# Encoder block in fp32 halves: output projection by token halves, FFN weight operands of four blocks kept in DRAM, a lead of six blocks

## The chip, the cores and the metric

The kernel runs on one core of one Trainium2 chip. The metric is the device time of one execution in microseconds, the median of several runs. PE is TensorE, DVE VectorE, ACT ScalarE, POOL GpSimd, and SP the engine that issues every DMA of this kernel, in order.

## The reference

One encoder layer on 1024 tokens of 1024 features, then a final norm. What the change touches is the middle of it:

```python
merged = gates[:, :, 0] * br_att + gates[:, :, 1] * br_sgu
h = h + merged @ w_out[l]
hn = rmsnorm(h, norm_ffn[l])
g, up = jnp.split(hn @ w_ffn_in[l], 2, axis=-1)
h = h + (jax.nn.silu(g) * up) @ w_ffn_out[l]
return rmsnorm(h, norm_final)
```

`w_out` is 1024 x 1024, `w_ffn_in` 1024 x 5632 (gate and up, 2816 columns each), `w_ffn_out` 2816 x 1024.

## The kernel before

Features lie on the 128 partitions, tokens along a row. A tile of 1024 features is 8 tiles of 128 (`KB`), a token half is 512 columns (`HALF`), and the FFN's 2816 columns are 22 blocks of 128 (`FB`).

**Products.** Every float32 operand is split into a high part (a cast by ACT into fp32r) and a low part (the difference, a subtraction by DVE or POOL). A product then is three matmuls of 128 x 128 by 128 x 512: high by high, high by low, low by high. `passes` (L158) and `multiply` (L175) issue them.

**The output projection** (L1193 to L1252) makes eight row blocks `j` of 128 features by two token halves: 16 products of 24 matmuls, in the hand-written order `order_w` (L1221), where halves alternate at first. `load_w` and `split_w` (L1034, L1039) fetch `w_out` and split it, half of the low parts on POOL and half on DVE. `collect_w` (L1202) adds the product to the residual row `h[j]` on DVE; `finish_row` (L1172) squares it on ACT and adds the square into `acc[half]`, mostly on POOL, and stores the row into `h_dram` once both halves are there. Once the eight rows of half 0 are collected, PE sums the squares (`sum_features`, L266), `inverse_rms` (L250) makes the reciprocal root with a power on POOL and three DVE instructions, and PE spreads it over the partitions (`spread`, L273) into `bc`. `first_operands` (L1214) then norms half 0 into `exact` and splits it into the right-hand operands `b11` and `b21`.

**The FFN's input product** uses seven products per block instead of eight (a Strassen-Winograd scheme over 2 x 2 halves: features by tokens on the right, features by gate and up on the left). `order` (L1109) lists them: products "1" and "2" use `b11` and `b21`, which come of token half 0 alone; "5", "6", "3", "7", "4" use `t1`, `t2`, `b22`, `t3`, `t4`, which need half 1 too. Products 1 and 2 of the first four blocks (`AHEAD`) lead, eight products; then the rest follows block by block, 154 products of 12 matmuls in all. `prepare_to(n)` (L1137) makes the weight operands up to product `n`: a combination on DVE for 5, 6, 3 and 7 (`combine`, L1132), a cast on ACT (L1156), and the low part on POOL (L1162) or, from block 4 on, for the products in `VECTOR_LO` on DVE (L173). They lie in four pairs of buffers of two products each, turn by turn in `fpool` and `wpool`. `load_raw` (L1119) fetches the raw rows.

The loop at L1400 goes through the products: it prepares four ahead, issues the product, and `collect` (L1272) takes it out of PSUM. Behind product 0 stand the sums of half 1, behind product 1 the spread; from then on `TAKE_F[i]` (L32) tells how many items of `other_operands` (L1314) follow product `i`. There are 20 items: four each for t1, t2, b22, t3 and t4, with a norm or difference on DVE, a cast on ACT and a low part, alternately on POOL and DVE (`put_later`, L1318).

**The FFN's output product** needs weight operands too, made early: `weights_g` (L1357) makes 84 of them during the input product, one item per product from `MAKE_FROM` (18) on, and keeps them in `g_dram`; they are loaded back later.

**Space.** `slots` (L58) has 36 buffers of 4 KB a partition for nearly everything. Tiles are allotted in program order, and an instruction that writes a reused buffer waits for its last user. PSUM has eight banks of 512 columns for products (`dense_ps`, L79). The order of each engine's work is the order of the program.

Of the kernel before, what the change touches and what calls it, by code (L numbers as in the profile page):

```python
# [16 lines left out]
P = 128  # L17
# [14 lines left out]
TAKE_F = (0, 2, 1, 2, 0, 2, 3, 2, 2, 4, 2, 1)  # L32
TAKE_G = (0, 2, 1, 1, 1, 3, 2, 2, 2, 2, 2, 1, 1, 1, 1, 1, 1, 2, 1, 1, 2, 0, 3)
POOL_LO = (0, 2, 6)
VECTOR_LO = "1247"
MAKE_FROM = 18
# [12 lines left out]
def encoder_block(ctx: ExitStack, tc: tile.TileContext, xT, w_in, w_v, w_vs, w_att, w_sgu, w_out,  # L49
# [984 lines left out]
    def load_w(j):  # L1034
        pool = wpool if j in (0, 2) else fpool if j in (4, 6) else None
        raws_w[j] = slot(f"wo{j}") if pool is None else pool.tile([P, D], F32, name=f"wo{j}", tag="raw")
# [71 lines left out]
    AHEAD = 4  # L1108
# [11 lines left out]
    def load_raw(f, i):  # L1120
        name = f"f{'gu'[i]}{f}"
        pool = (fpool, wpool)[i if f < 2 else 1 - f % 2]
        t = slot(name) if 2 <= f < AHEAD else pool.tile([P, D], F32, name=name, tag="raw")
        nc.sync.dma_start(t, w_ffn_in[i * FB + f])
        raws.setdefault(f, []).append(t)
# [11 lines left out]
    def prepare_to(n):  # L1137
        while state_f["next"] < min(n, len(order)):
            i = state_f["next"]
            p, f = order[i]  # L1140
            if i % 2 == 0:
                parts[i // 2] = weight_parts(f"w{i}", (fpool, fpool, wpool, wpool)[i // 2 % 4])
            (g0, g1), (u0, u1) = ((x[:, :HALF], x[:, HALF:]) for x in (raws[f][0], raws[f][-1]))
# [10 lines left out]
            c = slice(i % 2 * HALF, (i % 2 + 1) * HALF)  # L1154
            hi, lo = (x[:, c] for x in parts[i // 2])
# [7 lines left out]
            if (p, f) == ("7", 1):  # L1163
                load_pair(5)
            if p == "4" and (f == 1 or f > 3):
                load_pair(4 if f == 1 else f + 2)
            state_f["next"] += 1

    acc = [ftmp("acc0"), ftmp("acc1")]
    lazy = []  # L1170

    def finish_row(j, half, first=False, last=False):  # L1172
        x = h[j][:, halves[half]]
        if first:
            nc.scalar.activation(acc[half], x, AF.Square)
        else:
            q = tmp("sq")
            nc.scalar.activation(q, x, AF.Square)
            if last:
                do_lazy(99)  # L1180
            lazy.append(lambda: (nc.vector if last else nc.gpsimd).tensor_tensor(out=acc[half], in0=acc[half], in1=q, op=OP.add))
            if last:
                do_lazy(99)
        if half:
            nc.sync.dma_start(h_dram[j], h[j])

    def do_lazy(n):
        for _ in range(min(n, len(lazy))):
            lazy.pop(0)()
# [12 lines left out]
    def collect_w(j, half):  # L1202
        dst = h[j][:, halves[half]]
        nc.vector.tensor_tensor(out=dst, in0=dst, in1=banks_w.pop((j, half)), op=OP.add)  # L1204
        finish_row(j, half, first=j == 0, last=(j, half) in ((KB - 1, 0), (KB - 2, 1)))

    load_w(4)
    load_w(6)
    for j in range(KB):
        residual(j)  # L1210
        if j == 1:
            load_w(3)

    def first_operands(k):  # L1214
        if k % 4 == 0:
# [3 lines left out]
        put(("b11", "b21")[k // 4], k % 4, blk, nc.gpsimd if k in POOL_LO else nc.vector)  # L1219

    order_w = [(0, 0), (1, 0), (0, 1), (1, 1), (2, 0), (2, 1), (3, 0), (3, 1), (4, 0), (5, 0), (6, 0), (7, 0),  # L1221
               (4, 1), (7, 1), (5, 1), (6, 1)]
    ready_w = {0: 2, 3: 3, 5: 4, 6: 5, 7: 6, 8: 7}
    for i, (j, half) in enumerate(order_w):
        n = i - 12
        if i in ready_w:
            split_w(ready_w[i])
        if i == 1:
            load_w(5)
            load_w(7)  # L1230
# [4 lines left out]
        if i == 9:  # L1235
            for f in range(AHEAD):
                load_raw(f, 0)
            nc.scalar.activation(warm, ones, AF.Silu)
        if i == 10:
            load_raw(0, 1)  # L1240
            load_raw(1, 1)
        if n == 0:
            cols = inverse_rms("rms2_0", sum_features("ss2_0", acc[0], 4), 4)
        if n == 1:
            bc = dense_ps("bc2_0")
            spread(cols, bc, 4)
        collect_w(j, half)
        do_lazy(1)
        for k in ((), (0, 1), (2, 3, 4), (5, 6, 7))[n] if n >= 0 else ():
            first_operands(k)  # L1250
        if n >= 1:
            prepare_to((2, 3, 4)[n - 1])  # L1252
# [61 lines left out]
    def other_operands(bc):  # L1314
# [42 lines left out]
    def weights_g():  # L1357


        late_lo = []  # L1360

        def finish_lo():
            for n, t, src in late_lo:
                nc.vector.tensor_tensor(out=t[:, W3:2 * W3], in0=src, in1=t[:, :W3].bitcast(F32), op=OP.subtract)  # L1364
                nc.sync.dma_start(g_dram[n], t[:, :2 * W3].bitcast(F32))
            late_lo.clear()

        for c in range(PARTS):
            for r in range(4):
# [3 lines left out]
                yield 1  # L1373
                yield 1
                (a11, a12), (a21, a22) = ((t[:, :W3], t[:, W3:2 * W3]) for t in rows)
                kept = slot(f"gs{c}_{r}", (P, 2, HALF))
                s1, s3 = (kept[:, n, :W3] for n in range(2))
                for p in "1725634":
                    if p == "7":
                        nc.vector.tensor_tensor(out=s3, in0=a11, in1=a21, op=OP.subtract)  # L1380
                    elif p == "5":
                        nc.vector.tensor_tensor(out=s1, in0=a21, in1=a22, op=OP.add)
                    elif p == "6":
                        nc.vector.tensor_tensor(out=a11, in0=s1, in1=a11, op=OP.subtract)
                    elif p == "3":
                        nc.vector.tensor_tensor(out=a12, in0=a12, in1=a11, op=OP.subtract)
                    src = {"1": a11, "2": a12, "4": a22, "5": s1, "6": a11, "7": s3, "3": a12}[p]
                    n = order_g.index((c, r, p))
                    t = slot(f"g{n}", dt=F32R)
                    nc.scalar.copy(t[:, :W3], src)  # L1390
                    finish_lo()
                    late_lo.append((n, t, src))
                    yield 1
                finish_lo()
                yield 1
# [4 lines left out]
    for i in range(last_pair - 5):  # L1400
# [7 lines left out]
        if i == 1:  # L1408
# [4 lines left out]
        if i >= MAKE_FROM:  # L1413
            take(making, 1)
# [219 lines left out]
```

## Time and profile before

| what | value |
|---|---|
| median of 3 runs | 1350.84 us (1350.09 to 1350.95) |
| the profiled execution | 1349.5 us |
| its span, first to last instruction | 1347.8 us |
| mean granted TensorE clock, share of full | 0.992 |
| busy PE, DVE, ACT, POOL | 1312.0, 921.2, 571.8, 513.4 us |
| DMA moved | 179.42 MB, mean 133 GB/s |

Busy times are of the profiled execution. A matmul's duration overlaps the next one's, so the distance of two starts tells PE's pace, not the duration. The granted clock of a stretch is a mean over it, 1.00 for 2.4 GHz and 0.50 for 1.2 GHz.

### The profile page before, as it was taken

The page shows a single profiled execution, that of the slowest core. Times are in us where ns is not written, and L with a number is a line of the kernel's source. Part 1 is how long each engine was busy: PE and PEld are TensorE (multiplying, and loading weights), DVE is VectorE, ACT ScalarE, POOL GpSimd, SP SyncE. Part 2 cuts the span into 40 slices and gives each one's busy share as a digit, 9 for nine tenths or more (in the row PEclk, how much of TensorE's full clock was granted, in tenths as well). Part 3 has the DMA queues.
Part 4 walks back from the last instruction along what each step waited for, and adds up shares of the span by engine and source line. Part 5 has one row for each costly group of instructions (what it writes and reads, how often), then busy time and mean ns, then how long its engine had stood idle before and what let it go on. Part 6 is the DMA issues. An engine that isn't in the chain of part 4 may idle for free.

```text
span 1347.8 us, 17376 instructions
## 1 busy us (share of the span) xinstructions
PE 1312.0 (97%) x6290; PEld 1088.4 (81%) x6290; DVE 921.2 (68%) x1451; ACT 571.8 (42%) x1056; POOL 513.4 (38%) x402
## 2 busy tenths in 40 slices
PE   9999999999998999999987999999999999999997
PEld 7888888878886777888875788888888888888887
DVE  6257877771869778662279777788787857757445
ACT  7345666653334544432253344343344433212144
POOL 2425444414357355534367332212221232424332
PEclk9999999999999999999988999999999999999999
DMA  6001101012041121253111365666566558886723
GB/s 250 28 17 39 33 24 36 24 41 78 16 164 55 47 67 51 71 216 144 62 47 60 133 223 190 223 212 216 205 222 215 205 193 307 287 285 209 241 61 126
DMA packets 65782, 179.42 MB, mean 133 GB/s; under 512 B 7200, under 2 KB 10784, under 8 KB 65696
## 3 DMA queue, kind: packets, MB, share of 16 engines
q1 hardware_dynamic: 65696, 178.31, 38.6%
q8 instruction: 50, 0.82, 0.2%
q14 instruction: 36, 0.29, 0.1%
HBM read 125.33 MB, written 52.95 MB: 132 GB/s over the span
## 4 chain that ended last, share of the span: by engine, by line
PE 57%; DVE 5%; issue 1%; ACT 1%; POOL 0%; DMA 0%; DVEq 0%; ACTq 0%; POOLq 0%
PE c L182 41%; PE wo L1199 6%; PE mc L182 5%; PE last L168 3%; PE mp L182 2%; DVE s L1134 0%; DVE b L1347 0%; DVE t L1337 0%; DVE b22l L173 0%; DVE t L1330 0%; DMA g_dram<-g 0%; DVE b L1105 0%; DVE t2l L173 0%; DVE b22f L1105 0%; DVE mergedlo L781 0%
## 5 line engine op out<-in xcount | busy, mean ns | idle before, releaser
L1162 POOL TENSOR_TENSOR w_lo<-s,w_hi 128x512 fp32r<-128x512 f32 x70 | 106.0, 1519 | 270.9 <-ACT w_hi L1156 268.2
L182 PE MATMUL c<-t,g 128*128 128x512 f32 x432 | 103.1, 390 | 0.0
L1156 ACT CAST w_hi<-s 128x512 fp32r<-128x512 f32 x88 | 54.8, 622 | 109.5 <-DVE s L1134 106.7
L182 PEld LDWEIGHTS c<-t,g 128*128 128x128 f32 x432 | 80.9, 188 | 17.5 <-issue 0.4
L1481 DVE TENSOR_TENSOR h_all<-h_all,c 128x512 f32<-128x512 f32 x72 | 49.1, 686 | 52.2 <-PE c L182 51.3
L182 PE MATMUL c<-b,g 128*128 128x512 f32 x324 | 78.3, 389 | 0.0
L182 PEld LDWEIGHTS c<-b,g 128*128 128x128 f32 x324 | 60.8, 188 | 12.7
L504 ACT ACTIVATE p<-p,low 128x640 f32<-128x640 f32 (+4 forms) x64 | 44.7, 698 | 58.5 <-DVE low L496 58.3
L156 POOL TENSOR_TENSOR wm_lo<-wg,wm_hi 128x512 fp32r<-128x512 f32 x21 | 30.1, 1437 | 63.9 <-ACT wm_hi L155 60.1
L1445 ACT CAST t<-stage 128x512 fp32r<-128x512 f32 x36 | 22.3, 624 | 73.5 <-DVE stage L1442 68.1
L173 POOL TENSOR_TENSOR t<-stage,t 128x512 fp32r<-128x512 f32 x18 | 26.8, 1492 | 61.3 <-ACT t L1445 57.0
L1199 PE MATMUL wo<-mergedhi,wo_hi 128*128 128x512 f32 x128 | 50.0, 391 | 0.0
L1199 PE MATMUL wo<-mergedhi,wo_lo 128*128 128x512 f32 x128 | 49.8, 389 | 0.0
L1199 PE MATMUL wo<-mergedlo,wo_hi 128*128 128x512 f32 x128 | 49.8, 389 | 0.0
L496 DVE CUSTOM_DVE_ANT_0 p<-s,bias 128x640 f32<-128x640 f32 (+4 forms) x64 | 41.7, 652 | 10.7 <-PE s L492 8.9
L522 DVE TENSOR_TENSOR ptl<-t,pth 128x640 fp32r<-128x640 f32 (+4 forms) x64 | 41.7, 651 | 4.5 <-ACT pth L521 4.2
L168 PE MATMUL last<-act_hi,fo 128*128 128x256 f32 (+1 forms) x192 | 43.8, 320 | 0.0
L1390 ACT CAST g<-fo 128x384 fp32r<-128x384 f32 x60 | 30.6, 510 | 30.0 <-issue 14.8
L506 DVE TENSOR_SCALAR p<-p,inv 128x640 f32<-128x640 f32 (+4 forms) x64 | 39.6, 619 | 2.2
L1364 DVE TENSOR_TENSOR g<-fo,g 128x384 fp32r<-128x384 f32 x60 | 40.9, 681 | 0.0
L1204 DVE TENSOR_TENSOR h<-h,wo 128x512 f32<-128x512 f32 x16 | 11.0, 687 | 41.5 <-PE wo L1199 41.5
L515 PE MATMUL t<-ident,p 128*128 128x128 f32 x240 | 37.0, 274 | 1.8 <-DVE ptl L522 1.6
(425 smaller groups left out, 4256.1 us busy)
## 6 DMA issues: line engine op xcount, KB each, us to landing
g_dram<-g SPq DMA_DIRECT2D x84, 384.0 KB, 2.5
g<-g_dram SPq DMA_DIRECT2D x84, 384.0 KB, 3.6
fg<-in_w_ffn_in SPq DMA_DIRECT2D x22, 512.0 KB, 4.7
fu<-in_w_ffn_in SPq DMA_DIRECT2D x22, 512.0 KB, 4.2
act_dram<-u SPq DMA_DIRECT2D x44, 256.0 KB, 2.4
stage<-act_dram SPq DMA_DIRECT2D x22, 512.0 KB, 6.3
fo<-in_w_ffn_out SPq DMA_DIRECT2D x24, 384.0 KB, 4.3
xn<-in_xT SPq DMA_DIRECT2D x8, 512.0 KB, 7.6
```

What stands on the lines that cost most here:

```text
L168: nc.tensor.matmul(ps, w, x[:, s], start=k == 0 and i == 0, stop=k == kc - 1 and i == 2)
L182: nc.tensor.matmul(ps, w[:, ws], x, start=first and k == 0 and n == 0, stop=k == last and n == 2, skip_group_check=True)
L496: nc.vector.tensor_tensor_reduce(out=p[:, :w].rearrange("p (a c) -> p a c", a=parts), in0=ps[:, :parts, :c], in1=bias.rearrange("p (a c) - ...
L504: nc.scalar.activation(e["p"], e["p"], AF.Exp, bias=e["low"], scale=-1.0, accum_out=e["tot"])
L506: nc.vector.tensor_scalar(e["p"], e["p"], e["inv"], None, op0=OP.mult)
L515: nc.tensor.transpose(ps[:, b * P:(b + 1) * P], e["p"][:, b * P:(b + 1) * P], ident)
L522: nc.vector.tensor_tensor(out=lo[:, :w], in0=ps[:, :w], in1=hi[:, :w].bitcast(F32), op=OP.subtract)
L1156: nc.scalar.copy(hi, src)
L1162: nc.gpsimd.tensor_tensor(out=lo, in0=src, in1=hi.bitcast(F32), op=OP.subtract)
L1199: nc.tensor.matmul(banks_w[j, half], w, x, start=k == 0 and n == 0, stop=k == KB - 1 and n == 2, skip_group_check=True)
L1364: nc.vector.tensor_tensor(out=t[:, W3:2 * W3], in0=src, in1=t[:, :W3].bitcast(F32), op=OP.subtract)
L1481: nc.vector.tensor_tensor(out=dst, in0=dst, in1=banks_g[name, r], op=OP.add)
```

## The change

It does five things. The projection makes all eight rows of token half 0 first and then those of half 1 (in the order 6, 7, 0 to 5), collects a product one step later, and gives all low parts and square sums to DVE, at a distance of two operations (`later`, `split_later`). Meanwhile `weights_f` makes the 28 weight operands of FFN blocks 0 to 3 (`MADE`), three items per projection product, each 512 KB stored in `f_dram`; `products_of` is the body of the old `weights_g`, now shared. `prepare_to` loads these operands by two DMAs each instead of making them. Six blocks lead instead of four (`AHEAD`), so twelve products stand ahead; sums and spread of half 1 stand behind products 1 and 3. `TAKE_F` is thinner, the low parts of `other_operands` are all DVE's, and `weights_g` begins at product 32, with a second item at each eighth product.

```diff
-TAKE_F = (0, 2, 1, 2, 0, 2, 3, 2, 2, 4, 2, 1)
+TAKE_F = (0, 0, 0, 1, 1, 1, 1, 1, 1, 1, 2)
-POOL_LO = (0, 2, 6)
-MAKE_FROM = 18
+MAKE_FROM = 32
+MADE, AHEAD = 4, 6
...
     def split_w(j):
-        hi, lo = two_slots(f"wo_{j}") if j == 0 else weight_parts(f"wo_{j}", fpool if j in (3, 4, 7) else wpool)
+        hi, lo = two_slots(f"wo_{j}") if j in (0, 3, 4, 5) else weight_parts(f"wo_{j}", fpool if j > 5 else wpool)
         parts_w[j] = dict(hi=hi, lo=lo)
         for n, s in enumerate(halves):
-            split((hi[:, s], lo[:, s]), raws_w[j][:, s], nc.vector if n else None)
+            if j < 2:
+                split((hi[:, s], lo[:, s]), raws_w[j][:, s], nc.vector if n else None)
+            else:
+                split_later((hi[:, s], lo[:, s]), raws_w[j][:, s])
+
+    late_w = []
+
+    def later(n, *op):
+        late_w.extend(op)
+        while len(late_w) > n:
+            out, x, y, kind = late_w.pop(0)
+            nc.vector.tensor_tensor(out=out, in0=x, in1=y, op=kind)
+
+    def split_later(dst, src):
+        hi, lo = dst
+        nc.scalar.copy(hi, src)
+        later(2, (lo, src, hi.bitcast(F32), OP.subtract))
...
+            if f < MADE:
+                while low_f:
+                    put_low(low_f)
+                for m, part in enumerate((hi, lo)):
+                    nc.sync.dma_start(part.bitcast(F32), f_dram[f, int(p) - 1][:, halves[m]])
+                continue
...
-            if f >= AHEAD and p in VECTOR_LO and i < len(order) - 1:
+            if p in VECTOR_LO and i < len(order) - 1:
...
-            lazy.append(lambda: (nc.vector if last else nc.gpsimd).tensor_tensor(out=acc[half], in0=acc[half], in1=q, op=OP.add))
+            later(2, (acc[half], acc[half], q, OP.add))
...
+    def products_of(name, rows, width, put, sums):
+        late_lo = []
+
+        def finish_lo():
+            for p, t, src in late_lo:
+                nc.vector.tensor_tensor(out=t[:, width:2 * width], in0=src, in1=t[:, :width].bitcast(F32), op=OP.subtract)
+                put(p, t[:, :2 * width].bitcast(F32))
+            late_lo.clear()
+
+        yield 1
+        yield 1
...
+            t = slot(f"{name}_{p}", dt=F32R)
+            nc.scalar.copy(t[:, :width], src)
+            finish_lo()
+            late_lo.append((p, t, src))
+            yield 1
+        finish_lo()
+        yield 1
...
+    def weights_f():
+        for f in range(MADE):
+            yield from products_of(f"fw{f}", rows_f.pop(f), HALF,
+                                   lambda p, t: nc.sync.dma_start(f_dram[f, int(p) - 1], t),
...
-        put(("b11", "b21")[k // 4], k % 4, blk, nc.gpsimd if k in POOL_LO else nc.vector)
+        split_later([x[k % 4 // 2][:, k % 2] for x in right[("b11", "b21")[k // 4]]], blk)
...
+    order_w = [(j, 0) for j in range(KB)] + [(j, 1) for j in (6, 7, 0, 1, 2, 3, 4, 5)]
+    making = weights_f()
     for i, (j, half) in enumerate(order_w):
+        n = i - KB
+        if i in (1, 2):
+            later(0)
+            load_w(i + 5)
+        if i < 6:
+            split_w(i + 2)
+        if i in (0, 4, 8):
+            load_rows_f(i // 4 + 1)
...
         product_w(j, half, (KB - 1,) if i < 2 else range(KB))
         if i == 9:
             nc.scalar.activation(warm, ones, AF.Silu)
+            load_pair(4)
+        if n == 1:
+            later(0)
             cols = inverse_rms("rms2_0", sum_features("ss2_0", acc[0], 4), 4)
+        if n == 2:
             bc = dense_ps("bc2_0")
             spread(cols, bc, 4)
+        if i:
+            collect_w(*order_w[i - 1])
+        for k in ((), (), (0,), (1, 2), (3,), (4, 5), (6,), (7,))[n] if n >= 0 else ():
             first_operands(k)
+        take(making, 3 if i else 0)
+        residual(i + 1)
+        if n in (3, 5):
+            prepare_to(4 if n == 3 else 7)
+    collect_w(*order_w[-1])
+    later(0)
+    drain(making)
+    load_pair(5)
...
-            low.append((nc.vector if k % 2 else nc.gpsimd, lo, src, hi.bitcast(F32)))
+            low.append((nc.vector, lo, src, hi.bitcast(F32)))
...
-        if i == 0:
-            load_raw(2, 1)
-            load_raw(3, 1)
+        if i == 1:
             cols = inverse_rms("rms2_1", sum_features("ss2_1", acc[1], 4), 4)
-        if i == 1:
+        if i == 3:
             bc = dense_ps("bc2_1")
...
         if i >= MAKE_FROM:
-            take(making, 1)
+            take(making, 1 + (i % 8 == 0))
```

## Rows read from the trace of the kernel before

**Rows 1.** PE's share of the span, from the page's first part

```profile
PE 1312.0 (97%) x6290; PEld 1088.4 (81%) x6290; DVE 921.2 (68%) x1451; ACT 571.8 (42%) x1056; POOL 513.4 (38%) x402
```

**Rows 2.** chain that ended last, in order of time: start us, us, what

```profile
586.66 70.72 PE wo L1199 x312
...
769.02 379.11 PE c L182 x1671
...
1148.15 141.12 PE c L182 x621
```

**Rows 3.** timeline of PE, 674 to 733 us; brackets: idle before, and releaser

```profile
674.97 0.39 PE L182 MATMUL c<-b11h,w_hi 128*128 128x512 f32 x1
...
677.70 0.95 PE L270 MATMUL ss<-ones,acc 128*128 128x1 f32 x8
...
678.50 0.49 PE L182 MATMUL c<-b11h,w_hi 128*128 128x512 f32 x1
...
686.44 1.11 PE L276 MATMUL bc<-ident,rms_y 128*128 128x128 f32 x4 [4.92 <-DVE rms_y L263]
...
687.21 0.78 PE L182 MATMUL c<-b21h,w_hi 128*128 128x512 f32 x1
...
713.28 0.47 PE L182 MATMUL c<-b22h,w_hi 128*128 128x512 f32 x1 [2.48 <-ACT w_hi L1156]
...
718.94 0.47 PE L182 MATMUL c<-t3h,w_hi 128*128 128x512 f32 x1 [1.15 <-ACT w_hi L1156]
...
721.14 0.75 PE L182 MATMUL c<-t3l,w_hi 128*128 128x512 f32 x1 [1.03 <-DVE t3l L173]
...
731.01 0.47 PE L182 MATMUL c<-t4h,w_hi 128*128 128x512 f32 x1 [3.18 <-ACT w_hi L1156]
...
731.61 0.63 PE L182 MATMUL c<-t4h,w_lo 128*128 128x512 f32 x1
...
732.04 0.63 PE L182 MATMUL c<-t4h,w_hi 128*128 128x512 f32 x1
```

**Rows 4.** windows: stretch, us, busy of PE PEld DVE ACT POOL, clock, DMA share, GB/s

```profile
680.00:700.00 20.00, 15.08 (x61) 12.13 (x60) 15.69 (x22) 10.06 (x19) 13.29 (x10) 0.83 0.06 26
...
700.00:720.00 20.00, 16.37 (x64) 12.35 (x62) 19.17 (x19) 9.57 (x17) 16.24 (x10) 0.91 0.00 0
...
720.00:740.00 20.00, 15.66 (x54) 11.80 (x54) 18.72 (x20) 7.31 (x13) 11.96 (x9) 0.83 0.28 83
```

**Rows 5.** groups on DVE and POOL, 560 to 780 us, and one tile's operations

```profile
L1204 DVE TENSOR_TENSOR h<-h,wo 128x512 f32<-128x512 f32 x16 | 11.0, 687 | 41.5 <-PE wo L1199 41.5
...
L1181 DVE TENSOR_TENSOR acc<-acc,sq 128x512 f32<-128x512 f32 x2 | 1.4, 692 | 1.7 <-ACT sq L1178 1.7
...
L1105 DVE SCALAR_TENSOR_TENSOR exact<-h,vec,bc 128x512 f32<-128x512 f32 x8 | 5.7, 741 | 0.0
...
L1162 POOL TENSOR_TENSOR w_lo<-s,w_hi 128x512 fp32r<-128x512 f32 x18 | 27.7, 1542 | 28.5 <-ACT w_hi L1156 27.2 <-PE c L182 1.3
...
L173 DVE TENSOR_TENSOR t1l<-t,t1h x2: 679/1233/1787, 692.1 to 697.2; 128x512 fp32r<-128x512 f32 x2
```

**Rows 6.** windows inside the output projection, columns as in rows 4

```profile
600.00:620.00 20.00, 20.00 (x90) 16.57 (x89) 5.01 (x6) 3.97 (x7) 5.93 (x5) 1.00 0.48 189
...
620.00:640.00 20.00, 20.00 (x90) 16.53 (x90) 4.68 (x7) 7.12 (x12) 10.26 (x7) 1.00 0.49 182
```

**Rows 7.** DMA issues: KB each, median us to landing

```profile
g<-g_dram SPq DMA_DIRECT2D x84, 384.0 KB, 3.6
...
h<-in_xT SPq DMA_DIRECT2D x8, 512.0 KB, 8.7
```

**Rows 8.** windows late in the FFN, columns as in rows 4

```profile
1140.00:1160.00 20.00, 19.98 (x88) 16.09 (x87) 13.18 (x19) 3.67 (x6) 5.60 (x4) 1.00 1.03 402
...
1180.00:1200.00 20.00, 20.00 (x90) 16.56 (x89) 10.09 (x15) 3.74 (x6) 5.68 (x4) 1.00 0.89 308
```

**Rows 9.** window of the steady FFN, columns as in rows 4

```profile
1060.00:1080.00 20.00, 20.00 (x90) 16.57 (x89) 18.74 (x28) 9.24 (x19) 5.04 (x4) 1.00 0.61 214
```

More of the change, by code (lines that the diff above doesn't have):

```diff
@@ L1121, in load_raw @@
         name = f"f{'gu'[i]}{f}"
-        pool = (fpool, wpool)[i if f < 2 else 1 - f % 2]
-        t = slot(name) if 2 <= f < AHEAD else pool.tile([P, D], F32, name=name, tag="raw")
+        t = (wpool, fpool)[f % 2].tile([P, D], F32, name=name, tag="raw")
         nc.sync.dma_start(t, w_ffn_in[i * FB + f])
@@ L1142, in prepare_to @@
                 parts[i // 2] = weight_parts(f"w{i}", (fpool, fpool, wpool, wpool)[i // 2 % 4])
-            (g0, g1), (u0, u1) = ((x[:, :HALF], x[:, HALF:]) for x in (raws[f][0], raws[f][-1]))
+            c = slice(i % 2 * HALF, (i % 2 + 1) * HALF)
+            hi, lo = (x[:, c] for x in parts[i // 2])
+            state_f["next"] += 1
+            if f < MADE:
[4 more added lines that the diff above has]
+                continue
+            (g0, g1), (u0, u1) = ((x[:, :HALF], x[:, HALF:]) for x in raws[f])
             if p == "5":
@@ L1153, in prepare_to @@
                 src = {"1": g0, "2": g1, "4": u1}[p]
-            c = slice(i % 2 * HALF, (i % 2 + 1) * HALF)
-            hi, lo = (x[:, c] for x in parts[i // 2])
             nc.scalar.copy(hi, src)
@@ L1162, in prepare_to, with finish_row @@
                 nc.gpsimd.tensor_tensor(out=lo, in0=src, in1=hi.bitcast(F32), op=OP.subtract)
[L1163 to L1167, printed above, removed]
+            if p == "4":
+                load_pair(f + 2)
     acc = [ftmp("acc0"), ftmp("acc1")]
-    lazy = []
-    def finish_row(j, half, first=False, last=False):
+    def finish_row(j, half):
         x = h[j][:, halves[half]]
-        if first:
+        if (j, half) in (order_w[0], order_w[KB]):
             nc.scalar.activation(acc[half], x, AF.Square)
@@ L1204, in collect_w @@
         nc.vector.tensor_tensor(out=dst, in0=dst, in1=banks_w.pop((j, half)), op=OP.add)
-        finish_row(j, half, first=j == 0, last=(j, half) in ((KB - 1, 0), (KB - 2, 1)))
+        finish_row(j, half)
+    load_w(3)
+    residual(0)
     load_w(4)
[L1208 to L1212, printed above, removed]
+    load_w(5)
+    def products_of(name, rows, width, put, sums):
[7 more added lines that the diff above has]
+        yield 1
+        (a11, a12), (a21, a22) = ((t[:, :width], t[:, width:2 * width]) for t in rows)
+        s1, s3 = sums()
+        for p in "1725634":
+            if p == "7":
+                nc.vector.tensor_tensor(out=s3, in0=a11, in1=a21, op=OP.subtract)
+            elif p == "5":
+                nc.vector.tensor_tensor(out=s1, in0=a21, in1=a22, op=OP.add)
+            elif p == "6":
+                nc.vector.tensor_tensor(out=a11, in0=s1, in1=a11, op=OP.subtract)
+            elif p == "3":
+                nc.vector.tensor_tensor(out=a12, in0=a12, in1=a11, op=OP.subtract)
+            src = {"1": a11, "2": a12, "4": a22, "5": s1, "6": a11, "7": s3, "3": a12}[p]
+            t = slot(f"{name}_{p}", dt=F32R)
[5 more added lines that the diff above has]
+        yield 1
@@ new lines, in encoder_block, with load_rows_f @@
+    rows_f = {}
+    def load_rows_f(f):
+        rows_f[f] = []
+        for i in range(2):
+            name = f"m{'gu'[i]}{f}"
+            t = slot(name) if f % 2 else fpool.tile([P, D], F32, name=name, tag="raw")
+            nc.sync.dma_start(t, w_ffn_in[i * FB + f])
+            rows_f[f].append(t)
+    load_rows_f(0)
+    f_dram = dram.tile([MADE, 7, P, D], F32, name="f_dram")
+    def weights_f():
+        for f in range(MADE):
+            yield from products_of(f"fw{f}", rows_f.pop(f), HALF,
+                                   lambda p, t: nc.sync.dma_start(f_dram[f, int(p) - 1], t),
+                                   lambda: [fpool.tile([P, HALF], F32, name=f"fws{n}_{f}", tag="sum", bufs=3)
+                                            for n in range(2)])
@@ L1357, in weights_g @@
     def weights_g():
[L1360 to L1366, printed above, removed]
         for c in range(PARTS):
@@ L1372, in weights_g, with sums @@
                     nc.sync.dma_start(t[:, :2 * W3], w_ffn_out[j][:, c * 2 * W3:(c + 1) * 2 * W3])
[L1373 to L1395, printed above, removed]
+                def sums():
+                    t = slot(f"gs{c}_{r}", (P, 2, HALF))
+                    return t[:, 0, :W3], t[:, 1, :W3]
+                yield from products_of(f"gw{c}_{r}", rows, W3,
+                                       lambda p, t: nc.sync.dma_start(g_dram[order_g.index((c, r, p))], t), sums)
     others = iter(())
```

32 lines of the change are left out of this document (1 added, 31 removed).

## The prediction

> **What bounds the kernel now.** I read the page's engine line first: PE is busy 1312.0 of 1347.8 us [rows 1], so at most some 36 us of the span are PE's to win back. Next the chain that ended last, in order of time: from 769.02 us on it is PE alone, 1671 and then 621 products without a piece of another engine between [rows 2], and the last stage follows in the same manner. A microsecond saved before 769 therefore arrives at the end undiminished. The projection's own row gives PE's pace: 312 products in 70.72 us, 0.2267 us each, so one FFN product of 12 is 2.72 us [rows 2].
>
> Then PE's timeline between the two. The first FFN product begins at 674.97 [rows 3] and the dense run at 769.02 [rows 2]: 94.05 us. `order` puts 26 products of 12 into it (eight lead products, then 5, 6, 3, 7 of block 0 and on to the 7 of block 3), 26 x 2.72 = 70.7. So **23.3 us are lost** here. What the reader is to see in rows 3 is who released PE: before `bc` it is the chain of the second root (4.92 us idle), then a weight cast of ACT (2.48), again (1.15), a low part on DVE (1.03), and a cast again (3.18), 12.76 us together. The 8 small sums and 4 spreads cost about 1.1 (677.70 to 678.50 and 686.44 to 687.21, less one product's 0.23 each) [rows 3]. Most of the rest is a slower clock: the windows grant 0.83, 0.91 and 0.83 of 2.4 GHz from 680 to 740 [rows 4], that is stretches at 1.2 GHz behind each long idle, where successive products start 0.43 us apart (731.61, 732.04) instead of 0.2267 [rows 3].
>
> Why are casts late? In 700 to 740 DVE is busy 19.17 and 18.72 of 20 us [rows 4]: it makes the weight combinations of the first blocks (`prepare_to`) and the right-hand operands of the second token half (`other_operands`) at once, and ACT and POOL wait in line behind it. DVE's operations are slow there too: the same subtraction took 679 ns in one place and 1787 in another [rows 5], the long ones while POOL, whose low parts take 1542 ns each, is at work. In the projection, by contrast, DVE is busy only 5.01 and 4.68 us of 20 [rows 6]. That idle DVE is what the change spends.
>
> **The change, part by part.**
>
> *Weight operands of blocks 0 to 3, made early.* Each block has 4 combinations and 7 low parts on DVE and 7 casts on ACT: 44 and 28 in all. They leave the congested stretch and enter the projection, with 28 stores of 512 KB. They come back as two loads of 256 KB for each of the 28 products.
>
> DVE in the projection then holds 16 collects (687 ns), 14 square sums (692; 12 were POOL's), 12 low parts of `w_out` (half were POOL's), 44 operations of `making`, and 8 norms (741) with 8 low parts [rows 5]. At 0.69 us for what has no row of its own: 11.0 + 9.7 + 8.3 + 30.4 + 5.9 + 5.5 = 70.8 us of the projection's 384 x 0.2267 = 87.1. I take 0.69, the short end, because POOL is left with only the powers of the root. At the long end, 1.79 us for the 64 low parts and combinations, it would be 141 us and DVE would be the bound. Between the two I choose by the nearest row: `acc` and the norms in this same stage are at 692 and 741 [rows 5].
>
> By steps of 5.44 us (one product): steps 1 to 6 carry about 4.8 us, 10 to 13 about 5.6 with the norms. DVE also stands still at the first root from the end of product 9 for some 3.5 us. I work it forward to an end about 3 us behind the projection's last product. The first use of `b21` is two lead products (5.4 us) later and `ss2_1` stands there too, so I cost this at 0. No gain is possible here, since PE runs through the projection at its full pace already [rows 2]. If this cover of 2.4 us goes, each further us is one of PE.
>
> *PE's own waits in the projection.* The sums of half 0 stand behind product 9, though the half ends with product 7, and the spread behind product 10. Two products (10.9 us) cover the squares, one (5.4) the root. Sums and spreads are as many as before, so 0. Weights are split two products ahead: 0.
>
> *ACT's new waits.* `making` casts into slots that its own stores must free. I count 33 to 35 of 36 slots in use around steps 5 to 7. If a cast waits for a store, the next squares and `w_out` casts wait behind it, and DVE behind those. All `w_out` parts are cast by then and eight PSUM banks hold uncollected products, so nothing reaches PE: 0, with up to 5 us if the lag lasts to the roots.
>
> *SP's queue.* Each store waits on SP for DVE's low part, and behind it stand the residual loads, the stores of `h` and the operand loads. A residual row is collected two steps after its issue, 10.9 us minus the waits; such a load took 8.7 us in a crowded stretch [rows 7].
>
> *DMA volume in the projection.* 28 stores (14.7 MB), the rows of four blocks (4.2), 5 `w_out` (2.6), 8 residual rows in and 8 out (8.4), operands of the first seven products (3.7), block 4 (1.0): 34.6 MB. The same stage now has some 14 (5 `w_out`, 16 rows of `h`, 6 of block operands). At the 402 GB/s of the fullest window [rows 8] it takes 86 us of the 87. It fits with nothing to spare; halves of the stage differ (about 370 GB/s wanted in the first, more in steps 8 to 13, little in 14 and 15), and steps 14 and 15 take up the surplus. I cost it at 0 and keep a rival for it.
> By the Trainium skill (DMA: Bandwidth & Descriptors, section Specifications) a core's share of HBM is about 358 GB/s; by that the transfers last 96.6 us and the sum would be some 9.5 us worse. The trace moves 402 and so speaks against that limit on this single core.
>
> *Six blocks' products lead.* 12 products instead of 8 stand before the first that needs the other half: 32.6 us instead of 21.8. Loads of operands return in 3.6 us [rows 7] and are issued at least three products (8.2 us) ahead, so weights of made blocks should be in time. Only four hot operands (1 and 2 of blocks 4 and 5) are split there. The second root has no POOL queue before it and two lead products of cover: its 4.92 us go. The three waits on weight casts (2.48 + 1.15 + 3.18) go, with the clock behind them.
>
> *What is late next.* The 20 items of `other_operands` cost 30.6 us of DVE with POOL quiet (8 of t1 and t2 at 0.74 + 0.69 + 0.68, 4 of b22 at 0.68, 8 of t3 and t4 at 0.69 + 0.68) [rows 5]. t1, t2 and b22 end in the lead. By `TAKE_F` the last items of t3 are issued behind the collect of product 14, and those of t4 behind 16. Working DVE forward from the end of product 12, t3's last low part comes 4.1 us after product 14 ends (steps 12 and 13 put a collect, two differences and two low parts each on DVE, 3.4 us where PE takes 2.72, and step 14 again 3.4), and is wanted 2.3 us after, by the eleventh matmul of 15: 1.9 lost (rounded up). The same sum gives 1.9 before 17. So 3.8 us stay, between 0 (if DVE gets ahead) and the 5.4 of the stalls at these places now (1.15 + 1.03 + 3.18). For the clock I take one stretch at 1.2 GHz: eight products at 0.43 instead of 0.2267, 1.6 us, between none and two (3.2).
>
> *Later weights.* `weights_g` begins at product 32 instead of 18, with one extra item in eight, and so ends at about the same place. DVE has up to 18.74 us of work in 20 there [rows 9]; an eighth more of some 0.72 us for each product is 0.09 us. PE's run covers it: 0; uncovered it would be 0.09 x 109, 10 us.
>
> **Sum.** 23.3 now; left over are 1.1 (sums and spreads), 3.8 and 1.6: 6.5. Saved: 16.8 us. The profiled execution took 1349.5 us (span 1347.8 and 1.7 around it), 1.3 below the median; from the median, 1350.84 - 16.8 = 1334.0, **1334 us**.
>
> **Rivals.**
> - *The lead covers everything.* For it: 12 products last 32.6 us, and DVE needs 30.6. Against: items only begin behind product 3, and t3 and t4 are issued one or two per product. Then only 1.1 us stay lost: 1350.84 - 22.2 = 1328.6, 1329.
> - *The stall comes back elsewhere.* DVE ends the projection late, or a rotating slot or a queued load makes the lead wait. For it: 70.8 us of DVE work within 87 leave little. Price: half of what I count as won, about 8 us: 1342.
> - *Transfers bound the projection (the slower side).* Place: f_dram stores on SP, rows and residuals queued behind. At the 308 GB/s of another busy window [rows 8] 34.6 MB need 112.3 us, 25.3 beyond the stage: 1359. It turns the change into a loss below 34.6 MB / (87.1 + 16.8 us) = 333 GB/s. Against it: 402 GB/s over 20 us [rows 8], and 308 came with a DMA share of 0.89, so it was not full.
> - *Transfers at a middling rate.* A mix of stores and loads that reaches some 355 GB/s needs 97.5 us, 10 beyond the stage: 1344. The Trainium skill (DMA: Bandwidth & Descriptors, section Specifications) would put the time about there, with its 358 GB/s; the trace's 402 speaks against that rate as a limit.
> - *The change doesn't do what it says:* the early operands are made, but their loads come late at every lead product, and PE waits for DMA where it waited for ACT: 1351.
>
> **Numbers.** Forecast 55%; lead covers everything 15; stall elsewhere 12; slower by transfers 7; middling rate 6; no change 5. For this kernel 0.2% is 2.7 us, about what a measurement of it can tell from no change. Faster: 55 + 15 + 12 + 6 = 88, of which I give 1 to each other side for what I didn't see: 86; same 5; slower 9. The forecast alone spans 1330 (stalls nearly 0) to 1338 (two clock stretches, 5.4 of stalls). For 8 in 10 the range takes in the full cover and most of the returned stalls: 1329 to 1345.
>
> **What would show it.** Right: PE's products from the projection to the run after the lead without idle at `bc`; DVE near 16 of 20 us in the projection, its low parts at 0.6 to 0.7 us; DMA at 350 to 400 GB/s there; residual idle only at t3 and t4, released by DVE; a granted clock of 1.00 but for one stretch. Wrong: PE idle inside the projection or at the first lead products, released by DMA or by `b21`; DVE low parts above 1 us with POOL quiet; a time above 1345.

## The result, and the profile after

The changed kernel takes **1333.44 us** (median of 4 runs, 1332.85 to 1334.20) beside 1350.62 of the kernel before: a ratio of 0.9874 (95% interval 0.9856 to 0.9891). Its profiled execution took 1334.2 us, the longest of the four, with a span of 1332.5. The forecast was 1334, with a range of 1329 to 1345. In the table of runs below two medians take in one run each that lay far above the others (4665.88 us of e1, 7516.90 of e10); without these they are 1341.99 and 1333.27.

First the chain that ended last, in order of time (start us, us, what), through the projection and the lead. Where the chain of before is back on PE alone only from 769.02 us on [rows 2], this one stays on PE until 714.39, goes mostly through DVE, whose items of t3 and t4 come late, for 12.7 us, and is on PE again from 727.04.

```profile
586.38 54.40 PE wo L1207 x240
640.78 0.79 PE ss L270 x8
641.57 5.61 PE wo L1207 x24
647.17 0.44 PE bc L276 x4
647.61 27.25 PE wo L1207 x120
674.86 5.44 PE c L182 x24
680.30 0.79 PE ss L270 x8
681.09 5.61 PE c L182 x24
686.69 0.44 PE bc L276 x4
687.13 27.26 PE c L182 x120
...
727.04 121.49 PE c L182 x533
```

Sums and spreads stand between the products without a wait. PE's timeline shows what is left: the first FFN product, the four places where PE sat idle, and the first matmul of product 26 (counted from 0).

```profile
674.70 0.39 PE L182 MATMUL c<-b11h,w_hi 128*128 128x512 f32 x1
...
719.37 0.50 PE L182 MATMUL c<-t3l,w_hi 128*128 128x512 f32 x1 [0.69 <-DVE t3l L173]
...
720.58 0.50 PE L182 MATMUL c<-t3l,w_hi 128*128 128x512 f32 x1 [0.24 <-DVE t3l L173]
...
725.24 0.50 PE L182 MATMUL c<-t4l,w_hi 128*128 128x512 f32 x1 [0.22 <-DVE t4l L173]
...
727.04 0.50 PE L182 MATMUL c<-t4l,w_hi 128*128 128x512 f32 x1 [0.84 <-DVE t4l L173]
...
750.18 0.39 PE L182 MATMUL c<-t1h,w_hi 128*128 128x512 f32 x1
```

From 674.70 to 750.18 are 75.48 us for 26 products, as many as took 94.05 before [rows 2, 3]. Less 70.7 of work, **4.8 us are lost here instead of 23.3**. In place of the five releasers of [rows 3] stand DVE's low parts of t3 and t4 alone, and no weight cast.

The windows (columns as in [rows 4]) show both sides of the trade:

```profile
600.00:620.00 20.00, 20.00 (x90) 16.53 (x90) 15.86 (x26) 10.26 (x19) 0.00 (x0) 1.00 0.99 351
620.00:640.00 20.00, 20.00 (x90) 16.57 (x89) 11.36 (x18) 6.79 (x11) 0.00 (x0) 1.00 0.88 328
640.00:660.00 20.00, 20.00 (x96) 16.64 (x95) 16.98 (x31) 9.63 (x17) 1.02 (x1) 1.00 0.84 313
660.00:680.00 20.00, 20.00 (x90) 16.57 (x89) 15.33 (x25) 7.95 (x13) 0.00 (x0) 1.00 1.01 391
680.00:700.00 20.00, 20.00 (x96) 16.64 (x95) 13.28 (x24) 8.89 (x16) 1.01 (x1) 1.00 0.57 215
700.00:720.00 20.00, 19.32 (x86) 15.63 (x84) 15.05 (x25) 9.07 (x16) 0.00 (x0) 1.00 0.35 115
720.00:740.00 20.00, 18.69 (x80) 14.28 (x79) 11.46 (x18) 3.11 (x5) 0.00 (x0) 1.00 0.51 171
```

In the projection, from 600 to 640, DVE went from 5.01 and 4.68 us of 20 [rows 6] to 15.86 and 11.36, and DMA from 0.48 and 0.49 to 0.99 and 0.88. Behind it DVE fell from 19.17 and 18.72 [rows 4] to 15.05 and 11.46, POOL from 16.24 and 11.96 to nothing, and the granted clock is 1.00 where it was 0.91 and 0.83.

### The profile page after: what moved, and what is told of

The parts are those of the page before. It is cut to its first block, busy times and chain, and to the rows that moved or that the text cites. A ratio compares the mean times of both kernels' runs of the same rounds, so it can differ in the third digit from the quotient of the medians.

```text
span 1332.5 us, 17516 instructions
## 1 busy us (share of the span) xinstructions
PE 1308.0 (98%) x6290; PEld 1085.4 (81%) x6290; DVE 932.4 (70%) x1510; ACT 571.6 (43%) x1056; POOL 422.6 (32%) x343
## 4 chain that ended last, share of the span: by engine, by line
PE 58%; DVE 3%; DMA 1%; issue 1%; ACT 0%; POOL 0%; DVEq 0%; ACTq 0%; POOLq 0%
PE c L182 41%; PE wo L1207 7%; PE mc L182 5%; PE last L168 3%; PE mp L182 2%; DMA g<-g_dram 1%; DVE gw L1227 0%; DVE s L1148 0%; DVE mergedlo L781 0%; DVE t3l L173 0%; DVE exact L1411 0%; DVE gs L1239 0%; DVE u L1360 0%; PE bc L276 0%; ACT wm_hi L155 0%
## 5 line engine op out<-in xcount | busy, mean ns | idle before, releaser
L1183 POOL TENSOR_TENSOR w_lo<-s,w_hi 128x512 fp32r<-128x512 f32 x54 | 77.8, 1443 | 324.4 <-ACT w_hi L1177 324.4
L1177 ACT CAST w_hi<-s 128x512 fp32r<-128x512 f32 x72 | 44.7, 621 | 93.9 <-DVE s L1148 93.7
L260 POOL TENSOR_TENSOR rms_y<-rms_a,minus_half 128x4 f32<-128x4 f32 (+2 forms) x6 | 6.1, 1014 | 135.3 <-DVE rms_a L255 135.3
L1246 ACT CAST gw<-fo 128x384 fp32r<-128x384 f32 x60 | 30.4, 509 | 43.1 <-DMA fo<-in_w_ffn_out 19.2
L1227 DVE TENSOR_TENSOR gw<-fo,gw 128x384 fp32r<-128x384 f32 x60 | 42.2, 703 | 0.9 <-ACT gw L1246 0.8
L1357 ACT ACTIVATE g<-g 128x512 f32<-128x512 f32 x22 | 13.9, 633 | 62.8 <-DVE g L1356 62.8
```

The costliest lines, as they stand in the source:

```text
L1227: nc.vector.tensor_tensor(out=t[:, width:2 * width], in0=src, in1=t[:, :width].bitcast(F32), op=OP.subtract)
L1246: nc.scalar.copy(t[:, :width], src)
```

## The experiments

Two measures go with each run: the median of its runs, and the us lost between the first FFN product and product 26, which is the distance of their first matmuls on PE's timeline less 26 x 2.72. Each ratio is to the kernel before on the same chip. The medians of that kernel on the chips used are 1349.58 to 1350.62 us, and the change itself has 1333.44 and 1332.32 on two of them, so a difference of about 1 us between medians of two chips says nothing.

| run | median us | ratio to before (95%) | lost to product 26 |
|---|---|---|---|
| before | 1350.62 | 1 | 23.3 |
| the change | 1333.44 | 0.9874 (0.9856 to 0.9891) | 4.8 |
| e1, early weights, lead of four | 1342.13 | 0.9944 (0.9927 to 0.9961) | 13.7 |
| e2, lead of six alone | 1350.59 | 1.0013 (1.0004 to 1.0023) | 21.0 |
| e8, that, low parts of items on DVE | 1347.76 | 0.9989 (0.9979 to 0.9999) | 16.9 |
| e5, each early operand stored twice | 1352.43 | 1.0017 (1.0008 to 1.0027) | 9.9, and 11.7 in the projection |
| e11, half of them stored twice | 1334.60 | 0.9879 (0.9863 to 0.9895) | 5.6 |
| e6, 12 early low parts on POOL | 1333.64 | 0.9886 (0.9872 to 0.9901) | 4.7 |
| e10, half the items' low parts on POOL | 1333.51 | 0.9878 (0.9862 to 0.9895) | 4.9 |
| the change again | 1332.32 | 0.9874 (0.9857 to 0.9890) | 4.7 |
| e3, items two by two | 1331.42 | 0.9863 (0.9848 to 0.9877) | 3.0 |
| e4, extra item behind product 2 | 1331.80 | 0.9867 (0.9853 to 0.9882) | 4.7 |
| e7, e3 and e4 | 1330.24 | 0.9855 (0.9840 to 0.9869) | 3.0 |
| e9, e7 with hot low parts on POOL | 1331.65 | 0.9867 (0.9852 to 0.9882) | 3.8 |

**e1: is the longer lead needed?**

```diff
-TAKE_F = (0, 0, 0, 1, 1, 1, 1, 1, 1, 1, 2)
+TAKE_F = (0, 0, 0, 1, 1, 1, 1, 2, 3, 4, 4, 2, 2)
-MADE, AHEAD = 4, 6
+MADE, AHEAD = 4, 4
```

> The changed kernel with a lead of four blocks (8 products) instead of six; everything else stays, the items of other_operands are only moved up so that each operand is ready when it is used. Theory (the early weights alone are not enough: DVE needs the longer lead): from product 3 on DVE has 30.6 us of items and some 5 us of collects, 35.6 us, before the t4 product, which PE could reach after 10.9 + 5 x 2.72 = 24.5 us; so some 11 us of PE idle released by DVE's t and b22 low parts, and one or two stretches at 1.2 GHz: 8 to 14 us slower than the changed kernel, 1342 to 1347. Rival (the weight work was what clogged DVE, and with it gone the lead is idle comfort): within 3 us of the changed kernel, 1333 to 1337.

1342.13 us: about 9 slower than the change. PE's timeline has its longest waits at DVE's low parts of t2, b22 and t3, in order, and none at a weight:

```profile
703.34 0.50 PE L182 MATMUL c<-t2l,w_hi 128*128 128x512 f32 x1 [1.86 <-DVE t2l L173]
...
705.33 0.79 PE L182 MATMUL c<-t2l,w_hi 128*128 128x512 f32 x1 [1.02 <-DVE t2l L173]
...
709.21 0.50 PE L182 MATMUL c<-b22l,w_hi 128*128 128x512 f32 x1 [0.96 <-DVE b22l L173]
...
714.33 0.50 PE L182 MATMUL c<-t3l,w_hi 128*128 128x512 f32 x1 [1.75 <-DVE t3l L173]
```

The window 700 to 720 has a granted clock of 0.83 here and 1.00 in the change. So the change without the longer lead is worth some 8 us (7.5 against the kernel before on the same chip), and the rest is the lead's. e1 keeps the new order of the projection and the low parts on DVE, so these 8 us are not shown to be the early weights' alone; no run takes the three apart.

**e2 and e8: is the lead the whole gain?** e2 is the kernel before with `AHEAD = 6`, the thin `TAKE_F`, sums and spread behind products 1 and 3 and the late `weights_g`; gate rows of blocks 2 to 5 wait in slots and their pairs are loaded again.

```diff
-    AHEAD = 4
+    AHEAD = 6
...
-            if (p, f) == ("7", 1):
-                load_pair(5)
-            if p == "4" and (f == 1 or f > 3):
-                load_pair(4 if f == 1 else f + 2)
+            if p == "4":
+                raws[f + 2] = []
+                load_pair(f + 2)
```

> The kernel before with the lead of six blocks, the thin items and the late weights_g of the change, but no weight operand made early: the lead's twelve operands are split as PE goes, gate rows of blocks 2 to 5 wait in slots and are loaded a second time for the block's own products. Theory (both parts are needed): the long root stall (4.9 us) goes, but behind the lead DVE has combinations of block 0 and 1 besides t3 and t4, so casts of weights stay late: 10 to 16 us are lost between first FFN product and product 26 instead of 23.3, total 1338 to 1345. Rival (the lead is the whole gain): loss of 5 or less, 1332 to 1335.

1350.59 us: nothing gained, where I expected 6 to 13, and 21.0 lost where I expected 10 to 16. The wait at the second root shrinks from 4.92 us [rows 3] to 0.59, and most of what it gives comes back at b22, t3 and t4, on POOL:

```profile
688.80 0.65 PE L276 MATMUL bc<-ident,rms_y 128*128 128x128 f32 x4 [0.59 <-DVE rms_y L263]
...
718.15 0.47 PE L182 MATMUL c<-b22h,w_hi 128*128 128x512 f32 x1 [1.46 <-ACT w_hi L1155]
...
721.48 0.50 PE L182 MATMUL c<-b22l,w_hi 128*128 128x512 f32 x1 [1.48 <-POOL b22l L173]
...
726.03 0.80 PE L182 MATMUL c<-t3l,w_hi 128*128 128x512 f32 x1 [2.84 <-POOL t3l L173]
...
741.46 0.79 PE L182 MATMUL c<-t4l,w_hi 128*128 128x512 f32 x1 [3.63 <-POOL t4l L173]
```

The 2.3 us that are won before product 26 go again in the later products, which lose 3.3 us more than before, 1.74 of them in one wait for a weight cast; e2 has the late `weights_g`, so its 0 is not the lead's alone.

e8 takes POOL's half of these away, as the change does:

```diff
-            low.append((nc.vector if k % 2 else nc.gpsimd, lo, src, hi.bitcast(F32)))
+            low.append((nc.vector, lo, src, hi.bitcast(F32)))
```

> The kernel with the lead alone (no early weights), with one line more of the change: all low parts of other_operands on DVE instead of every other one on POOL. In the lead alone PE waited longest for POOL's low parts of t3 and t4 (2.8 and 3.6 us). Theory (two-engine sharing was the trouble, the lead is good once POOL is left to the weights): the loss before product 26 falls from 21.0 to 12 or less, 1339 to 1343. Rival (without the early weights DVE and ACT have too much to do in this stretch, whoever makes the low parts): the waits move to weight casts and DVE, loss 16 to 22, 1345 to 1351.

1347.76 us; the rival holds, in its size and in its place. The waits move to DVE and to casts, of which these are the longest two of PE, and DVE is full where it has hot weights and items together (the last row is a window, columns as in [rows 4]):

```profile
719.52 0.47 PE L182 MATMUL c<-b22h,w_hi 128*128 128x512 f32 x1 [1.53 <-ACT w_hi L1155]
...
725.81 0.80 PE L182 MATMUL c<-t3l,w_hi 128*128 128x512 f32 x1 [1.71 <-DVE t3l L173]
...
720.00:740.00 20.00, 13.71 (x45) 8.23 (x44) 19.65 (x25) 7.93 (x13) 7.74 (x5) 0.91 0.19 65
```

So the two parts of the change need each other: alone, each with the late `weights_g`, they give about 8 and 0 us, together 17.

**e5 and e11: how near are the transfers to their limit?** e5 stores every early operand a second time, into a DRAM tensor that nobody reads; e11 does so for blocks 1 and 3.

```diff
-                                   lambda p, t: nc.sync.dma_start(f_dram[f, int(p) - 1], t),
+                                   lambda p, t: [nc.sync.dma_start(x[f, int(p) - 1], t) for x in (f_dram, again)],
```

> The changed kernel, but each of the 28 early weight operands is stored twice, the second time to a DRAM tensor that nobody reads: 14.7 MB more in the output projection, 49.3 MB in all. Theory (34.6 MB was just within what the transfers carry, about 400 GB/s, and volume is the limit of this cover): 49.3 MB need 123 us, 36 more than the stage; a few us are hidden behind its end, so 20 to 36 us slower than the changed kernel, 1353 to 1370, with a DMA share near 1 through the projection and PE idle at its roots or in the lead. Rival (the order of waits, not the volume, sets when things come; or PE's cover is far larger than thought): under 10 us slower, below 1343.

1352.43 us, 19 slower than the change, just below the range that I gave. The trace has 16.8 of them between the projection's first matmul and product 26 (11.7 in the projection). In the projection the DMA share is 1 and PE waits, first for a low part of `w_out` and for the sums, both late behind DVE, whose collects waited 15.1 us for residual rows (6.5 in the change), then in the lead for loads of the early operands:

```profile
632.85 0.50 PE L1207 MATMUL wo<-mergedhi,wo_lo 128*128 128x512 f32 x1 [3.11 <-DVE wo_lo L1054]
...
651.50 1.87 PE L270 MATMUL ss<-ones,acc 128*128 128x1 f32 x8 [3.59 <-DVE acc L1054]
...
703.61 0.47 PE L182 MATMUL c<-b21h,w_hi 128*128 128x512 f32 x1 [2.67 <-DMA w_hi<-f_dram]
...
716.59 0.47 PE L182 MATMUL c<-b21h,w_hi 128*128 128x512 f32 x1 [1.64 <-DMA w_hi<-f_dram]
```

```diff
-                                   lambda p, t: nc.sync.dma_start(f_dram[f, int(p) - 1], t),
+                                   lambda p, t: [nc.sync.dma_start(x[f, int(p) - 1], t) for x in (f_dram, again)[:1 + f % 2]],
```

> The changed kernel with the 14 early operands of blocks 1 and 3 stored twice: 7.3 MB more, 42.0 MB in the projection, half of what the run with all stored twice added. There 14.7 MB more, 36 us at 405 GB/s, cost 19 us, so some 17 us of transfers were hidden by slack. If a fixed slack of that size comes first and volume counts beyond it: 18 us more of transfers cost 1 to 3 us, 1334 to 1336.5. If there is no slack and each MB has its price: half of 19, 9 to 10 us slower, 1342 to 1344.

1334.60 us, 1.2 slower than the change: the slack comes first. Between two chips 1.2 us would say nothing, but the trace agrees, with 0.6 us more in the projection and 0.8 more up to product 26. Its windows from 620 to 680 carry more than any window of the kernel before, with PE all but untouched:

```profile
620.00:640.00 20.00, 20.00 (x90) 16.55 (x89) 10.06 (x17) 5.29 (x9) 0.00 (x0) 1.00 1.01 403
640.00:660.00 20.00, 19.64 (x93) 16.08 (x92) 17.39 (x32) 11.02 (x19) 1.02 (x1) 1.00 1.02 412
660.00:680.00 20.00, 20.00 (x90) 16.57 (x89) 16.23 (x27) 8.08 (x13) 0.00 (x0) 1.00 1.02 404
680.00:700.00 20.00, 19.62 (x93) 15.81 (x91) 10.63 (x20) 7.77 (x15) 1.01 (x1) 1.00 1.00 383
```

**e6 and e10: does POOL's silence matter?** e6 gives POOL the low parts of products 1, 5 and 7 of the early operands, e10 every other low part of `other_operands`, as before the change.

```diff
-                nc.vector.tensor_tensor(out=t[:, width:2 * width], in0=src, in1=t[:, :width].bitcast(F32), op=OP.subtract)
+                (nc.gpsimd if width == HALF and p in "157" else nc.vector).tensor_tensor(out=t[:, width:2 * width], in0=src, in1=t[:, :width].bitcast(F32), op=OP.subtract)
```

> The changed kernel, but the low parts of products 1, 5 and 7 of the early weight operands (12 of 28) are made by POOL instead of DVE. Theory (DVE's operations last 0.69 us only while POOL is quiet, and are up to 1.8 us beside POOL): DVE gives up 12 x 0.69 = 8 us but its other operations in the projection grow to 0.8 to 1.3 us on average, so DVE ends later, not earlier; 0 to 6 us slower than the changed kernel, 1333 to 1340, and its DVE means in the projection above 0.8 us. Rival (POOL is free help): DVE means stay at 0.69, DVE busy falls by 8 us, time the same within 1 us.

1333.64 us. DVE's operations did get longer, by the groups of the projection (mean ns behind the comma), first of the change, then of e6:

```profile
L1227 DVE TENSOR_TENSOR fw<-mg,fw 128x512 fp32r<-128x512 f32 x16 | 11.0, 687 | 1.8 <-ACT fw L1246 1.4
L1054 DVE TENSOR_TENSOR acc<-acc,sq 128x512 f32<-128x512 f32 x14 | 9.6, 685 | 0.0
```

```profile
L1054 DVE TENSOR_TENSOR acc<-acc,sq 128x512 f32<-128x512 f32 x14 | 11.0, 786 | 0.1
...
L1227 DVE TENSOR_TENSOR fw<-mg,fw 128x512 fp32r<-128x512 f32 x12 | 9.6, 803 | 2.0 <-ACT fw L1246 1.9
```

So POOL's help was no relief: over the projection DVE is busy 68.0 us with 12 operations fewer, and 67.3 in the change, neither the 8 us less of the rival nor a later end that PE feels. The loss is 4.7 as in the change.

```diff
-            low.append((nc.vector, lo, src, hi.bitcast(F32)))
+            low.append((nc.vector if k % 2 else nc.gpsimd, lo, src, hi.bitcast(F32)))
```

> The changed kernel with one line undone: every other low part of other_operands on POOL, as before. Theory (POOL beside DVE lengthens both): DVE's own operations in the lead grow from 0.69 to 0.9 us and more on average, the low parts on POOL come 1.5 to 1.8 us after their cast, t3 and t4 are later: 3 to 8 us slower than the changed kernel, 1336 to 1341. Rival (DVE is the bound of the lead, and 10 of 20 low parts less are a relief): same or up to 3 us faster.

1333.51 us, where I expected 1336 to 1341. DVE's differences grow to 798 to 890 ns, but it has ten operations fewer, and its busy time up to product 26 is 43.1 us beside 45.2. The time is the rival's "same", but not its relief: with the weights out of the way, the lead bears either.

**e3, e4, e7, e9: what is still to be had.** The first three ran on one chip with the change itself.

> The changed kernel itself, unaltered, beside the next two on the same chip: what they are compared with. 1333 to 1334, some 4.7 us lost before product 26, about 2 in the later FFN products, and 0.5 to 1.8 in the output product.

1332.32 us (1331.80 to 1333.73), with 4.7 lost before product 26, and 1.0 in the later products.

```diff
-TAKE_F = (0, 0, 0, 1, 1, 1, 1, 1, 1, 1, 2)
+TAKE_F = (0, 0, 0, 1, 2, 2, 2, 2, 2, 2, 2, 2, 2, 1)
```

> The changed kernel with the same 20 items of other_operands taken two per product from product 4 on, instead of one until 9. Theory (the 3.2 us still lost before the t3 and t4 products are DVE's items coming too late, while DVE is busy only 13 of 20 us in the lead): those stalls go, 2 to 3.2 us faster than the changed kernel, 1330 to 1331.5. Rival (two items per product, 4.2 us of DVE in 2.72 of PE, delay the casts of the four hot weights or ACT's collects, and the loss moves into the lead): same time or slower, 1333 or more.

The waits at t3 and t4 are gone, and 3.0 us are lost instead of 4.7. Its median of 1331.42 is 0.9 below the change's, but the single runs overlap. Both had a part of the truth: two items per product hold up the low parts of two hot weights in the lead. The same two waits are there in e7:

```profile
701.86 0.50 PE L182 MATMUL c<-b11h,w_lo 128*128 128x512 f32 x1 [0.60 <-DVE w_lo L173]
...
705.22 0.50 PE L182 MATMUL c<-b21h,w_lo 128*128 128x512 f32 x1 [0.31 <-DVE w_lo L173]
```

```diff
-            take(making, 1 + (i % 8 == 0))
+            take(making, 1 + (order[i][0] == "2"))
```

> The changed kernel, but the second item of weights_g comes behind every product 2 (whose collect is ACT's) instead of every eighth product. Theory (the 2 us lost in the later FFN products are bursts of making that meet a loaded product): the waits there go, 1 to 2 us faster than the changed kernel, 1331.5 to 1332.5. Rival (the rate of making is the cause, wherever the extra item stands, or waits just move): within 0.7 us of the changed kernel.

The two waits in the later products that the next section shows are not in its trace, but one of them is missing from the trace of the change run beside it too. The median is 0.5 lower, within the spread, and 1.0 us is lost in the later products as in that run, so whether it helps stays open.

> The changes of the two runs before together. If both theories hold their gains add: 3 to 5 us faster than the changed kernel, 1328.5 to 1330.5, and only the sums and spreads (0.9 us) stay lost before product 26. If one of them falls, only the other's gain is there.

**1330.24 us** (1329.98 to 1330.46), 2.1 below the change on the same chip, with all runs of one below all of the other: it beats both kernels. The time is in the range expected, but 2.1 is short of the 3 to 5 us, and 3.0 stay lost before product 26 instead of 0.9.

```diff
-            if p in VECTOR_LO and i < len(order) - 1:
+            if f >= AHEAD and p in VECTOR_LO and i < len(order) - 1:
```

> The run with both improvements (items two by two, extra item behind product 2), where PE still loses 1.2 us to DVE's low parts of two hot weights in the lead; here POOL, idle in the lead, makes the low parts of the four hot weights. If the waits go and DVE is little slowed: 1 us faster, 1329 to 1329.7. If POOL's 1.3 to 1.8 us a piece slow DVE's items, as they do elsewhere, t3 and t4 are late again: 0 to 3 us slower, 1330 to 1333.

1331.65 us on another chip, and 3.8 lost where e7 loses 3.0, so no gain: the two waits go, and one of 1.64 us appears, released by ACT's copy of a product. t3 and t4 are not late, as the second branch had it; it is before them that two of DVE's differences, beside low parts on POOL, take 1.79 and 1.80 us.

```profile
708.82 0.50 PE L182 MATMUL c<-b21h,w_hi 128*128 128x512 f32 x1 [1.64 <-ACT sg L1346]
```

## Why the prediction was right

**The place and the mechanism.** The 23.3 us lay where [rows 3, 4] put them, and 18.5 of them came back, 1.7 more than forecast. The span fell by 15.3; the difference went to later products (below), a term put at 0. So that the time came within 0.6 us of the forecast is partly luck: one miss of 1.7 us and one of some 3.5 point opposite ways, and the medians fell by 17.2 where the two profiled executions differ by 15.3.

**The sum, term by term.** Left over should be 6.5: sums and spreads 1.1, DVE's late t3 and t4 3.8, one stretch at 1.2 GHz 1.6. Measured are 1.4 (0.81 for the sums, 0.36 for the spread, 0.27 of slower spacing just behind), 3.2 (1.5 in the t3 product, 1.7 in the t4 product, the slower spacing just behind each wait included) and 0, with 0.1 elsewhere. The 1.1 was read too low: the sums begin where the next product would have begun (674.97 + 2.72 = 677.69 [rows 3]), so nothing comes off, and before they and the spread cost 0.80 and 0.77. The waits of 12.76 leave out one of 0.71 just before 769.02, released by DVE. The clock term was sized too high: with idle pieces of up to 0.84 us the granted clock stayed at 1.00, while the windows with pieces of 1.03 to 4.92 us had 0.83 to 0.91 before [rows 3, 4]. The length of a piece does not decide it alone: e2 and e8 have one of 1.09 and 1.08 us at the same place, and their windows 680 to 700 grant 1.00 and 0.91.

**The terms costed at nothing.** DVE at the short end of 0.69 held (683 to 687 ns), and so did the cover of the roots: both spreads stand in the chain without a wait. DVE was busy 67.3 us in the projection, forecast 70.8; it waited 6.5 us for residual rows behind SP's queue there, and none of it reached PE. Later weights were the one term at 0 that cost something. In the later products up to the last of the input products 2.3 us are lost now, under 0.1 before, most of it in two waits:

```profile
862.63 0.47 PE L182 MATMUL c<-b22h,w_hi 128*128 128x512 f32 x1 [0.52 <-ACT w_hi L1177]
...
931.95 0.50 PE L182 MATMUL c<-b21h,w_hi 128*128 128x512 f32 x1 [1.06 <-ACT sg L1346]
```

The second is behind an operation of `weights_g` on DVE that took 1.65 us, beside a low part on POOL, where others take 0.55, and that held up ACT's next copy. It is not in every execution: in the change's second profile the first wait is there (0.52) and the second is not, and 1.0 us is lost. The output product lost 1.7 us instead of 0.4, with a wait of 0.37 for a load of `g_dram`; that too was 0.4 in the second profile, so it is not shown to be the change's.

**The transfers.** I said that 34.6 MB fit with nothing to spare. That was too narrow. Over the whole projection (586 to 675) the change moved 352 GB/s at a share of 0.94, which makes 31 MB; the rest lay outside. e11 moved 393 GB/s there, and 383 instead of 215 from 680 to 700: by these rates 3.9 of its 7.3 MB more went into the projection and 3.4 behind it. That is where the slack was, and e11 used about all of it, since loads of early operands begin to be late (one wait of 0.38 us). By e5, volume decides at some 17 to 19 us of transfers beyond what the change moves (36 more, for 19 us by the medians or 17 by the trace). The rival on the slower side was the right mechanism with its point of decision put too near.

By the Trainium skill (DMA: Bandwidth & Descriptors, section Specifications) a core's share of HBM is about 358 GB/s. The run e11 moved 403 to 412 GB/s over 60 us on this core alone, so that figure was no limit here.

**The rivals.** The lead covered the roots and weights, not t3 and t4. A returned stall showed only with one of the parts left out (e1, e2, e8). My picture of POOL as what slows DVE was right for the durations. In the changed kernel they cost no time (e6, e10), because DVE has room. In the kernel before they were much of what filled DVE. These are the windows from the first FFN product to product 26, before and after (columns as in [rows 4]):

```profile
674.97:769.02 94.05, 80.45 (x326) 63.55 (x324) 76.11 (x91) 36.52 (x65) 55.93 (x37) 0.91 0.22 73
```

```profile
674.70:750.18 75.48, 73.49 (x326) 59.38 (x324) 45.24 (x73) 22.92 (x40) 1.01 (x1) 1.00 0.56 195
```

DVE had 91 operations of 0.84 us on average, with POOL busy 55.93 us, and has 73 of 0.62 with POOL idle. At 0.62 the 91 would take 56 us, so by this estimate 20 of the 31 us that DVE got free come from its shorter operations, and 11 from those that moved elsewhere. The change brings both at once, since POOL's low parts moved too. A kernel that only quiets POOL was not run; by the same estimate DVE with POOL's 37 operations besides its 91 would need 79 us, more than the 70.7 of PE's work.

## What to carry to other kernels

Work that stalls the bound engine at a stage border can be made earlier, where another engine idles, and parked in DRAM; but count what remains at the border against the time that independent products give there. Neither the early weights (8 us) nor the longer lead (0) was worth its half: one empties the queue, the other buys time for what is still in it. When an engine is full, look at the mean duration of its operations besides their number: here two thirds of what DVE got free came with POOL's silence. When stores that nobody awaits fill the transfers, add a dummy store to learn how much slack there is before calling them the bound.

## What the runs showed of the hardware

A DVE addition or subtraction of 128x512 with both inputs in float32 took 0.68 to 0.69 us on average in the projection and the lead of the change, with POOL idle. With POOL making 12 low parts in the projection (e6), the means of its groups there went up to 0.96 us, some staying at 0.68. In the kernel before single ones took 1.75 to 1.78 us beside low parts on POOL of 1.7 us (707 to 717 us). The transfers carried up to 419 GB/s over 20 us of mixed loads and stores (e5, 640 to 660), at a DMA share of 1.03. Single idle pieces of PE of 0.84 us (the change), 1.64 us (e9) and 2.67 us (e5, with one of 1.64 behind it) left the granted clock of their windows at 1.00; with one of 1.08 us in e8 it was 0.91.
